# One denominator pass for eight attention heads instead of two passes for four, in a two-layer hybrid decoder trunk

## The chip, the cores and the metric

The kernel runs on one core of one Trainium2 chip. The metric is the device time of one execution in microseconds; of several runs the median is given. PE is the matrix engine, DVE the vector engine, ACT the scalar engine, POOL and SP the other two.

## What is computed

Two layers. Each is a half SwiGLU, a mixer of four branches (sliding-window attention, a short gated convolution, "native sparse attention", retention), and another half SwiGLU. The change touches the softmax of the two attention branches. Cut to it:

```
def masked_softmax(s, mask, sink=None):
    s = jnp.where(mask, s, -inf); m = max(s); (sink: m = max(m, sink))
    p = exp(s - m); denom = sum(p); (sink: denom += exp(sink - m))
    return p / max(denom, 1e-30)

for each block of 128 queries and each of 8 heads (2 groups of 4 heads share keys and values):
    o = masked_softmax(q @ k.T * scale, mask, sink) @ v
merged = sum over branches of sigmoid(gate_i) * (y_i @ W_branch_i);   x = x + merged @ w_out
```

With 512 tokens the selected blocks of the sparse branch are all blocks, so its "selected" and "window" parts are both causal attention over the keys so far, and each is weighted by a gate per head.

## The kernel before

Tokens are four blocks of 128 (`NT`). All large matmuls run as sums of products of a rounded part and a remainder of the operands (`whi`, `wlo` from `split`: ACT makes `whi` at L214, DVE makes `wlo` at L215), so each weight tile costs one ACT and one DVE instruction before PE can use it.

The sliding-window branch (`swa`) calls `soft` once for each token block, the sparse branch (`nsa`) twice for each (selected, then window, with 1 to 4 key blocks), so a layer has 12 calls. For a head, `scores` makes two matmuls into a PSUM bank `sc` (two banks; L1057, L1058), DVE adds the mask, scales and takes the extreme (L1072) into a tile `P` (nine buffers), and ACT takes the exponential and its sum (L1073). The sums of four heads stand in a tile `dn` of 128x4; DVE bounds it (L1080), inverts it (L1082), in `nsa` multiplies it by the gate (L1084), in `swa` first adds the sink's term (L1077 to L1079), and then scales the four P (L1086). This is `soft_g`, called for group 0 and then group 1.

`pv_acc` then transposes P in key blocks (`turn(j)`: four transposes of group 0 into one PSUM bank `tp`, four of group 1 into the other, L1095), ACT copies each bank to a tile `PT` (three buffers, L1099), and PE multiplies by the values into the bank `pv` (L1108). The transposes of a group at j = 0 wait by hand (`together`) for the last scaling of that group. At the end of a token block `put_y` rounds `pv` (ACT, L851) and takes the remainder (DVE, L852).

Which instruction stands where on each engine is decided by a scheduler when the program is built, from priorities in the order of the code and its own estimate of when things are ready. Every engine then works through its fixed order. What fills PE between the steps of the attention is `merge`: gate projections (L232) and branch matmuls (L834), and on DVE L807, L838 and L839 behind them. In `nsa` the work at hand is `merge(3, yd)`, the retention branch. `merge(2, yc)`, the sparse branch itself, can only start when `nsa` has ended, and w_out and the second SwiGLU follow it. Its L834 read `E` (the rounded part, from L851) and `y` (the remainder, from L852).

Of the kernel before, what the change touches and what calls it, by code (L numbers as in the profile page):

```python
# [13 lines left out]
OP = mybir.AluOpType  # L14
# [58 lines left out]
def body(tc, ins, out):  # L73
    nc = tc.nc
    pe, dve, act, pool, sp = nc.tensor, nc.vector, nc.scalar, nc.gpsimd, nc.sync
    L = ins["w_in"].shape[0]
    es = ExitStack()
# [7 lines left out]
    def sc_t():  # L85
        return pp.tile([128, 512], F32, name="sc", tag="sc", bufs=2)

    def tp_t():
        return pp.tile([128, 512], F32, name="tp", tag="tp", bufs=2)
# [75 lines left out]
    def small(shape, dt=F32, name="sm", bufs=6):  # L165
        n = int(np.prod(shape[1:]))
        return (ph.get("mx") or wp).tile([shape[0], n], dt, name=name, tag=name, bufs=bufs)
# [530 lines left out]
    def mixer(l, spill, F):  # L698
# [12 lines left out]
        def p_t():  # L711
            return aq.tile([128, 512], F32, name="P", tag="P", bufs=9)
# [4 lines left out]
        G, o, oq = {}, 0, 0  # L717
        for nm, a in (("swa_q", ins["swa_q_gain"][l]), ("swa_k", ins["swa_k_gain"][l]),
                      ("nsa_q", ins["nsa_q_gain"][l]), ("nsa_k", ins["nsa_k_gain"][l].rearrange("a b -> (a b)")),
                      ("sink", ins["swa_sinks"][l])):  # L720
            n = a.shape[0]
# [10 lines left out]
        nsink = small([128, 8], name="nsink", bufs=1)  # L732
# [20 lines left out]
        mark, pv_last, scaled, ahead = {}, [None], {}, {}  # L753

        def together(first, ready):

            tc.add_manual_dep(first.ins, ready.ins.name, SYNC, reason="together")
# [296 lines left out]
        def scores(i, qT, kT, h, s0, n):  # L1054
            g, q = h // 4, qT[h][:, i * 128:(i + 1) * 128]
            ps = sc_t()
            pe.matmul(ps[:, :n], q, kT[0][:, g, s0:s0 + n], start=True, stop=False)  # L1057
            pe.matmul(ps[:, :n], q, kT[1][:, g, s0:s0 + n], start=False, stop=True)  # L1058
            return ps

        def soft(i, qT, rr, kT, s0, n, mask, wts, sink):

            return [p for g in range(2) for p in soft_g(g, i, qT, rr, kT, s0, n, mask, wts, sink)]

        def soft_g(g, i, qT, rr, kT, s0, n, mask, wts, sink):
            nm = small([128, 4], name="nm", bufs=4)
            dn = small([128, 4], name="dn", bufs=4)
            P = []
            for h in range(4):
                ps = scores(i, qT, kT, 4 * g + h, s0, max(n, 256))  # L1070
                p = p_t()
                dve.tensor_tensor_reduce(p[:, :n], ps[:, :n], mask, rr[:, i, 4 * g + h:4 * g + h + 1], nsink[:, 4 * g + h:4 * g + h + 1] if sink else 3e38, OP.add, OP.min, nm[:, h:h + 1])  # L1072
                act.activation(p[:, :n], p[:, :n], AF.Exp, bias=nm[:, h:h + 1], scale=-1.0, accum_out=dn[:, h:h + 1])  # L1073
                P.append(p)
            if sink:
                e = small([128, 4], name="es", bufs=4)
                dve.tensor_tensor(e, nm, G["sink"][:, 4 * g:4 * g + 4], op=OP.add)  # L1077
                act.activation(e, e, AF.Exp)
                dve.tensor_tensor(dn, dn, e, op=OP.add)  # L1079
            dve.tensor_scalar(dn, dn, 1e-30, None, op0=OP.max)  # L1080
            w = small([128, 4], name="w8", bufs=4)
            dve.reciprocal(w, dn)  # L1082
            if wts is not None:
                dve.tensor_tensor(w, w, wts[:, 4 * g:4 * g + 4], op=OP.mult)  # L1084
            for h in range(4):
                scaled[g] = dve.tensor_scalar(P[h][:, :n], P[h][:, :n], w[:, h:h + 1], None, op0=OP.mult)  # L1086
            return P

        def pv_acc(pv, P, nblk, V, first, last):
            def turn(j):  # L1090
                pts = []
                for g in range(2):
                    ps = tp_t()
                    for r in range(4):
                        t = pe.transpose(ps[:, r * 128:(r + 1) * 128], P[4 * g + r][:, j * 128:(j + 1) * 128], ident)  # L1095
                        if r == 0 and j == 0:
                            together(t, scaled[g])
                    pt = aq.tile([128, 512], F32, name="PT", tag="PT", bufs=3)
                    last_copy[0] = act.activation(pt, ps, AF.Copy)  # L1099
                    pts.append(pt)  # L1100
                return pts, last_copy[0]

            last_copy = [None]
            pts, copied = turn(0)
            for j in range(nblk):
                nxt = turn(j + 1) if j + 1 < nblk else (None, None)
                for g in range(2):
                    pv_last[0] = pe.matmul(pv[g * 64:(g + 1) * 64], V(g, j), pts[g], start=first and j == 0, stop=last and j == nblk - 1)  # L1108
                    if g == 0:

                        together(pv_last[0], copied)
                pts, copied = nxt
# [4 lines left out]
        def swa(qT, rr, V, kT):  # L1117
            y = y_tiles()
            for i in range(NT):
                s0, n = (max(i - 1, 0) * 128, 256 if i else 128)  # L1120
                mask = C["band"] if i else C["band"][:, 128:]
                P = soft(i, qT, rr, kT[0], s0, n, mask, None, True)
                pv = pv_t()
                b0 = max(i - 1, 0)
                pv_acc(pv, P, n // 128, lambda g, j: V(0, g, b0 + j), True, True)
                mark["swa"] = pv_last[0]
                put_y(pv, y, i)
            return y
# [75 lines left out]
        def nsa(gates):  # L1204
# [8 lines left out]
            for i in range(NT):  # L1213
# [35 lines left out]
                for ty in range(2):  # L1249
                    P = soft(i, qT, rr, kT[ty], 0, n, mask, g3[:, i, :, 1 + ty], False)  # L1250
                    pv_acc(pv, P, i + 1, lambda g, j, ty=ty: V(ty, g, j), False, ty == 1)
# [134 lines left out]
    for l in range(L):  # L1386
        E = early(l)
        ffn_run(F, (E,))
        E.go(None, st["made"].ins)
        ph["two"] = False  # L1390
        leave("hp")
        leave("fp")
        F = ffn(*weights(2, l), norm_end, to_next(l))
        mixer(l, spills[l], F)
        enter("hp", "left")
        nxt = ffn(*weights(1, l + 1), norm_end, to_mix(l + 1)) if l < L - 1 else None
        ffn_run(F, nxt)
        F = nxt
# [30 lines left out]
```

## Time and profile before

| what | value |
| --- | --- |
| median of 3 runs | 2732.51 us (2730.71 to 2732.75) |
| profiled execution: time, span | 2731.97 us, 2729.9 us |
| PE busy | 2705.9 us (99%), 17303 matmuls |
| DVE busy | 2086.9 us (76%), 3474 instructions |
| ACT busy | 1346.8 us (49%), 2136 instructions |
| DMA | 291 MB, mean 107 GB/s |

The time is the span plus 2.1 us around it. Busy shares are means over stages that differ: the sliding-window stages lie at about 550 to 610 and 1900 to 1960 us, the sparse-attention stages at 835 to 965 and 2190 to 2315 us, and the rest is the two SwiGLUs, projections and retention. A PE that is busy is not always at its peak, as the ends of matmuls are modelled.

### The profile page before, as it was taken

Reading aid. Unit: us, or ns where it says so; the run is one execution under the profiler, and the core shown is the slowest. Engines: PE = TensorE matmul, PEld = TensorE weight load, DVE = VectorE, ACT = ScalarE, POOL = GpSimd, SP = SyncE. Lnnn points to the kernel's source line nnn. Section 1 sums busy time; section 2 is a strip of 40 time slices with the busy share of each in tenths; the row PEclk is TensorE's granted clock in tenths of the full one; section 3 lists DMA queues with packets and bytes.
Section 4 is the critical chain, followed back from the end, with each engine's and each line's share of the span. In section 5 each row is a group of like instructions: output and inputs, shape, how many; then the busy total and the mean of one; then the engine's idle time right before and its main releaser. Section 6 shows DMA issues by size and latency. Waiting matters only on the chain.

```text
span 2729.9 us, 42548 instructions
## 1 busy us (share of the span) xinstructions
PE 2705.9 (99%) x17303; PEld 2368.0 (87%) x17303; DVE 2086.9 (76%) x3474; ACT 1346.8 (49%) x2136; POOL 65.0 (2%) x70
## 2 busy tenths in 40 slices
PE   8999999999999999999999999999999999999999
PEld 7999999978877679999899999998788776899997
DVE  8887799674858779786897868996658587788774
ACT  7444565463336655443554435655532465554442
POOL 0000010000000010000000000000000000100000
PEclk8999999999999999999999999999999999999999
DMA  5223423523332152323323333344232323332322
GB/s 172 93 89 112 132 97 129 183 83 114 91 124 63 35 182 82 120 86 101 124 78 111 98 101 125 108 154 149 74 110 91 110 62 97 120 109 93 115 72 77
DMA packets 243335, 291.24 MB, mean 107 GB/s; under 512 B 8060, under 2 KB 211652, under 8 KB 241092
## 3 DMA queue, kind: packets, MB, share of 16 engines
q1 hardware_dynamic: 235604, 273.78, 30.8%
q0 software_dynamic: 3136, 12.59, 1.4%
q8 instruction: 135, 2.21, 0.3%
q10 hardware_dynamic: 4400, 2.17, 0.3%
q14 instruction: 60, 0.49, 0.1%
HBM read 269.64 MB, written 18.87 MB: 106 GB/s over the span
## 4 chain that ended last, share of the span: by engine, by line
PE 85%; issue 10%; DVE 2%; ACT 2%; DMA 1%; POOL 0%; ACTq 0%; POOLq 0%; DVEq 0%
PE sc L437 23%; PE mm L567 16%; PE tp L437 12%; PE mm L232 7%; PE pv L437 6%; PE mm L834 5%; PE mm L786 3%; PE mm L1312 3%; PE pv L1108 2%; PE tp L1095 2%; PE sc L1057 1%; PE pv L786 1%; PE sc L1058 1%; DMA rawd<-in_ffn_w_down_dram 0%; PE sc L1158 0%
## 5 line engine op out<-in xcount | busy, mean ns | idle before, releaser
L214 ACT ACTIVATE whi<-raw 128x1024 fp32r<-128x1024 f32 (+2 forms) x338 | 333.7, 989 | 563.8 <-PE mm L567 122.6
L215 DVE TENSOR_TENSOR wlo<-raw,whi 128x1024 fp32r<-128x1024 f32 (+2 forms) x338 | 381.6, 1134 | 160.3 <-ACT whi L214 154.1
L567 PE MATMUL mm<-h,whi 128*128 128x512 f32 x1408 | 442.9, 395 | 0.2 <-DVE h L554 0.2
L214 ACT ACTIVATE whi<-s 128x1024 fp32r<-128x1024 f32 x232 | 245.8, 1060 | 337.6 <-PE tp L437 83.6
L215 DVE TENSOR_TENSOR wlo<-s,whi 128x1024 fp32r<-128x1024 f32 x232 | 282.7, 1220 | 48.6 <-ACT whi L214 48.0
L567 PEld LDWEIGHTS mm<-h,whi 128*128 128x128 f32 x1408 | 259.9, 188 | 59.6 <-DVE h L554 0.6
L437 PE MATMUL sc<-E,whi 128*128 128x256 f32 x1856 | 295.9, 281 | 0.0
L567 PE MATMUL mm<-h,wlo 128*128 128x512 f32 x704 | 277.9, 395 | 0.0
L437 PEld LDWEIGHTS sc<-E,whi 128*128 128x128 f32 x1856 | 253.1, 190 | 0.4 <-ACT sn L424 0.4
L437 PE MATMUL sc<-E,wlo 128*128 128x256 f32 x928 | 186.3, 282 | 0.0
L571 DVE SCALAR_TENSOR_TENSOR XT<-mm,XT 128x512 f32<-128x512 f32 x128 | 88.1, 688 | 124.8 <-PE mm L567 124.8
L437 PE MATMUL sc<-Ahi,whi 128*128 128x256 f32 x816 | 165.5, 284 | 3.3 <-ACT whi L214 3.3
L232 PE MATMUL mm<-Ahi,whi 128*128 128x512 f32 x416 | 165.2, 397 | 0.0
L232 PE MATMUL mm<-Ahi,wlo 128*128 128x512 f32 x416 | 164.7, 396 | 0.0
L437 PE MATMUL sc<-Ahi,wlo 128*128 128x256 f32 x816 | 164.1, 283 | 0.5 <-DVE wlo L215 0.5
L437 PE MATMUL sc<-Alo,whi 128*128 128x256 f32 x816 | 164.2, 283 | 0.0
L232 PE MATMUL mm<-Alo,whi 128*128 128x512 f32 x416 | 164.1, 394 | 0.0
L567 PEld LDWEIGHTS mm<-h,wlo 128*128 128x128 f32 x704 | 132.0, 187 | 32.2
L214 ACT ACTIVATE whi<-rawd 128x1024 fp32r<-128x1024 f32 (+1 forms) x96 | 94.7, 988 | 131.3 <-PE sc L437 66.1
L437 PE MATMUL tp<-E,whi 128*128 128x256 f32 x928 | 148.1, 281 | 0.0
L437 PEld LDWEIGHTS sc<-E,wlo 128*128 128x128 f32 x928 | 143.3, 190 | 0.2 <-DVE wlo L215 0.2
L443 DVE TENSOR_TENSOR s<-s,raw 128x1024 f32<-128x1024 f32 x116 | 141.4, 1219 | 0.9
(321 smaller groups left out, 6036.6 us busy)
## 6 DMA issues: line engine op xcount, KB each, us to landing
raw<-in_w_in_dram SPq DMA_DIRECT2D x66, 1024.0 KB, 5.8
raw<-in_ffn_w_gate_dram SPq DMA_DIRECT2D x44, 1024.0 KB, 5.3
raw<-in_ffn_w_up_dram SPq DMA_DIRECT2D x44, 1024.0 KB, 7.8
rawd<-in_ffn_w_down_dram SPq DMA_DIRECT2D x32, 1024.0 KB, 5.4
rawd<-in_ffn_w_down_dram SPq DMA_DIRECT2D x16, 768.0 KB, 4.4
gs<-O SPq DMA_DIRECT2D x8, 1024.0 KB, 4.0
raw<-in_w_branch_dram SPq DMA_DIRECT2D x8, 1024.0 KB, 7.5
raw<-in_w_branch_dram SPq DMA_DIRECT2D x16, 512.0 KB, 8.8
```

Of the source, the lines that this page charges most:

```text
L214: act.activation(hi, src, AF.Copy)
L215: dve.tensor_tensor(lo, src, fv(hi), op=OP.subtract)
L232: pe.matmul(ps, x, y, start=first and j == 0, stop=last and j == len(passes) - 1)
L437: pe.matmul(ps[:, g * 256:(g + 1) * 256], x[:, g * 4 + c], factor(u, s, c), start=first and n == 0, stop=last and n >= 22, skip_group_chec ...
L443: dve.tensor_tensor(t, a, b, op=OP.add)
L567: pe.matmul(ps, x[:, k, j * 128:(j + 1) * 128], h[:, s, b], start=k == 0 and n == 0, stop=k == nf - 1 and n == 2)
L571: dve.scalar_tensor_tensor(XT[d], ps, 0.5, XT[d], op0=OP.mult, op1=OP.add)
L786: pe.matmul(ps[i][:, :n], a, w, start=kk == 0 and j == 0, stop=kk == KT - 1 and j == 2)
L834: pe.matmul(ps, x[:, k], v[:, k], start=k == 0 and j == 0, stop=k == 3 and j == 2)
L1095: t = pe.transpose(ps[:, r * 128:(r + 1) * 128], P[4 * g + r][:, j * 128:(j + 1) * 128], ident)
L1108: pv_last[0] = pe.matmul(pv[g * 64:(g + 1) * 64], V(g, j), pts[g], start=first and j == 0, stop=last and j == nblk - 1)
L1312: pe.matmul(ps, x[:, k], v, start=k == 0 and j == 0, stop=k == KT - 1 and j == 2)
```

## The change

The maxima, the sums, the reciprocals and the weights of all eight heads of a block now stand in tiles of 128x8. The instructions on them are issued once for eight heads, after the last exponential, and all eight P are scaled behind them. The first transposes of both groups wait for the last of the eight scalings, so the eight of j = 0 stand together. The three small tiles have three buffers in place of four. Below the change the lines of the kernel move up by three (L1095 becomes L1092, L1086 becomes L1083, L1108 becomes L1105).

```diff
         def soft(i, qT, rr, kT, s0, n, mask, wts, sink):
 
-            return [p for g in range(2) for p in soft_g(g, i, qT, rr, kT, s0, n, mask, wts, sink)]
-
-        def soft_g(g, i, qT, rr, kT, s0, n, mask, wts, sink):
-            nm = small([128, 4], name="nm", bufs=4)
-            dn = small([128, 4], name="dn", bufs=4)
+            nm = small([128, 8], name="nm", bufs=3)
+            dn = small([128, 8], name="dn", bufs=3)
             P = []
-            for h in range(4):
-                ps = scores(i, qT, kT, 4 * g + h, s0, max(n, 256))
+            for h in range(8):
+                ps = scores(i, qT, kT, h, s0, max(n, 256))
                 p = p_t()
-                dve.tensor_tensor_reduce(p[:, :n], ps[:, :n], mask, rr[:, i, 4 * g + h:4 * g + h + 1], nsink[:, 4 * g + h:4 * g + h + 1] if sink else 3e38, OP.add, OP.min, nm[:, h:h + 1])
+                dve.tensor_tensor_reduce(p[:, :n], ps[:, :n], mask, rr[:, i, h:h + 1], nsink[:, h:h + 1] if sink else 3e38, OP.add, OP.min, nm[:, h:h + 1])
                 act.activation(p[:, :n], p[:, :n], AF.Exp, bias=nm[:, h:h + 1], scale=-1.0, accum_out=dn[:, h:h + 1])
                 P.append(p)
             if sink:
-                e = small([128, 4], name="es", bufs=4)
-                dve.tensor_tensor(e, nm, G["sink"][:, 4 * g:4 * g + 4], op=OP.add)
+                e = small([128, 8], name="es", bufs=3)
+                dve.tensor_tensor(e, nm, G["sink"], op=OP.add)
                 act.activation(e, e, AF.Exp)
                 dve.tensor_tensor(dn, dn, e, op=OP.add)
             dve.tensor_scalar(dn, dn, 1e-30, None, op0=OP.max)
-            w = small([128, 4], name="w8", bufs=4)
+            w = small([128, 8], name="w8", bufs=3)
             dve.reciprocal(w, dn)
             if wts is not None:
-                dve.tensor_tensor(w, w, wts[:, 4 * g:4 * g + 4], op=OP.mult)
-            for h in range(4):
-                scaled[g] = dve.tensor_scalar(P[h][:, :n], P[h][:, :n], w[:, h:h + 1], None, op0=OP.mult)
+                dve.tensor_tensor(w, w, wts, op=OP.mult)
+            for h in range(8):
+                scaled[h // 4] = dve.tensor_scalar(P[h][:, :n], P[h][:, :n], w[:, h:h + 1], None, op0=OP.mult)
             return P
...
                         if r == 0 and j == 0:
-                            together(t, scaled[g])
+                            together(t, scaled[1])
```

The scheduler orders more than these lines anew. On PE, here is the last block of the sparse branch in layer 1 as it stands before, from the second run of transposes on (`tp<-ident,P` are transposes, `pv` the products with the values, `mm` the merge of the retention branch):

```order
L1095 MATMUL tp<-ident,P 128x128 x8
L232 MATMUL mm<-Ahi,wlo 128x512
L834 MATMUL mm<-E,whi 128x512 x2
L1095 MATMUL tp<-ident,P 128x128 x4
L1108 MATMUL pv<-PT,b_8029 64x512 x2
L1095 MATMUL tp<-ident,P 128x128 x4
L834 MATMUL mm<-E,wlo 128x512
L1095 MATMUL tp<-ident,P 128x128 x4
L1108 MATMUL pv<-PT,b_8029 64x512 x2
L1095 MATMUL tp<-ident,P 128x128 x4
L834 MATMUL mm<-E,whi 128x512
L1095 MATMUL tp<-ident,P 128x128 x4
```

The same place on PE with the change, from the last merge matmuls of the retention branch to the first two of the sparse branch (`y_7567` is its remainder):

```order
L834 MATMUL mm<-E,whi 128x512 x2
L834 MATMUL mm<-E,wlo 128x512
L1092 MATMUL tp<-ident,P 128x128 x16
L1105 MATMUL pv<-PT,b_7993 64x512 x2
L1092 MATMUL tp<-ident,P 128x128 x8
L1105 MATMUL pv<-PT,b_7993 64x512 x2
L1092 MATMUL tp<-ident,P 128x128 x8
L1105 MATMUL pv<-PT,b_7993 64x512 x4
L834 MATMUL mm<-E,whi 128x512
L834 MATMUL mm<-y_7567,whi 128x512
```

The merge matmuls between and behind the transposes are gone from there: all of the retention branch's stand ahead of the first transposes. Counted over the whole order from the last scores of `nsa` to its first merge matmul, 40 merge matmuls (L232, L834) stood there before and 14 do now; the other 26 stand ahead of the last scores. Layer 2 has the same counts.

On DVE, the end of the same block before (`w_9191` holds the weights of the second four heads, `mm` in L838 is a merge product):

```order
L838 SCALAR_TENSOR_TENSOR th<-th,mm 128x512
L839 TENSOR_TENSOR merged<-merged,th 128x512
L1080 TENSOR_SCALAR dn<-dn 128x4
L1082 RECIPROCAL w_9191<-dn 128x4
L1084 TENSOR_TENSOR w_9191<-w_9191,cg 128x4
L1086 TENSOR_SCALAR P<-P,w_9191 128x512 x4
L215 TENSOR_TENSOR wlo<-raw,whi 128x1024
L807 TENSOR_TENSOR th<-mm,R 128x512
L852 TENSOR_TENSOR y_7603<-pv,E 128x4x128
```

And with the change, behind the eighth L1069 (the mask and maximum of the last head, L1072 before):

```order
L807 TENSOR_TENSOR th<-mm,R 128x512
L215 TENSOR_TENSOR wlo<-raw,whi 128x1024
L1077 TENSOR_SCALAR dn<-dn 128x8
L1079 RECIPROCAL w_9103<-dn 128x8
L838 SCALAR_TENSOR_TENSOR th<-th,mm 128x512
L1081 TENSOR_TENSOR w_9103<-w_9103,cg 128x8
L839 TENSOR_TENSOR merged<-merged,th 128x512
L215 TENSOR_TENSOR wlo<-raw,whi 128x1024
L1083 TENSOR_SCALAR P<-P,w_9103 128x512 x8
L852 TENSOR_TENSOR y_7567<-pv,E 128x4x128
```

Between the reciprocals and the scalings now stand L838, L839 and a split of weights. That L838 reads the product `mm` of the last merge matmuls of the retention branch, those ahead of the sixteen transposes.

## Rows read from the trace of the kernel before

**Rows 1.** Busy time by engine in the sparse stage of layer 1.
```profile
core 0: us, PE busy (x) PEld busy (x) DVE busy (x) ACT busy (x) POOL busy (x), PEclk, DMA share, GB/s
835.00:965.00 130.00, 129.24 (x658) 87.34 (x657) 98.39 (x329) 81.75 (x203) 4.52 (x8) 1.00 0.24 68
```

**Rows 2.** Groups by shape: busy us, mean ns, then idle time before them.
```profile
L1082 DVE RECIPROCAL w<-dn 128x4 f32<-128x4 f32 x48 | 8.4, 175 | 0.9
L1080 DVE TENSOR_SCALAR dn<-dn 128x4 f32<-128x4 f32 x48 | 8.0, 166 | 3.6 <-ACT P L1073 3.3
```

**Rows 3.** Timeline, layer 1: last scores to the second transposes; start us, us, engine.
```profile
942.48 0.40 PE L1058 MATMUL sc<-b,b 128*128 128x512 f32 x1
...
943.88 0.60 PE L1095 MATMUL tp<-ident,P 128*128 128x128 f32 x4
...
944.23 0.48 PE L232 MATMUL mm<-Alo,whi 128*128 128x512 f32 x1
...
944.55 0.39 PE L232 MATMUL mm<-Ahi,wlo 128*128 128x512 f32 x1
...
944.78 0.40 PE L232 MATMUL mm<-Ahi,whi 128*128 128x512 f32 x1
...
944.88 0.74 DVE L1072 CUSTOM_DVE_ANT_0 P<-sc,cst,rr 128x512 f32<-128x512 f32 x1
...
947.49 1.67 DVE L1086 TENSOR_SCALAR P<-P,w 128x512 f32<-128x512 f32 x4
...
949.34 1.04 PE L1095 MATMUL tp<-ident,P 128*128 128x128 f32 x8
...
950.13 0.48 PE L232 MATMUL mm<-Ahi,wlo 128*128 128x512 f32 x1
...
950.45 0.63 PE L834 MATMUL mm<-E,whi 128*128 128x512 f32 x2
```

**Rows 4.** Timeline, layer 1: first product with the values to the first sparse merge.
```profile
951.72 1.08 PE L1108 MATMUL pv<-PT,b 128*64 128x512 f32 x4
...
952.89 0.60 ACT L1099 ACTIVATE PT<-tp 128x512 f32<-128x512 f32 x1 [1.32 <-PE pv L1108]
...
953.54 0.66 PE L1095 MATMUL tp<-ident,P 128*128 128x128 f32 x4
...
958.44 1.08 PE L1108 MATMUL pv<-PT,b 128*64 128x512 f32 x4
...
961.16 0.50 PE L834 MATMUL mm<-E,whi 128*128 128x512 f32 x1 [0.28 <-ACT whi L214]
```

**Rows 5.** Groups by shape in 940 to 962 us, as in rows 2.
```profile
L214 ACT ACTIVATE whi<-raw 128x1024 fp32r<-128x1024 f32 x4 | 4.0, 1050 | 3.1 <-PE mm L232 3.1
...
L215 DVE TENSOR_TENSOR wlo<-raw,whi 128x1024 fp32r<-128x1024 f32 x2 | 2.4, 1222 | 1.5 <-ACT whi L214 1.5
L838 DVE SCALAR_TENSOR_TENSOR th<-th,mm 128x512 f32<-128x512 f32 x2 | 1.4, 684 | 0.0
L839 DVE TENSOR_TENSOR merged<-merged,th 128x512 f32<-128x512 f32 x1 | 0.7, 692 | 0.0
```

**Rows 6.** Timeline, layer 2: last scores, last values, rounding, first sparse merge.
```profile
2291.63 0.39 PE L1058 MATMUL sc<-b,b 128*128 128x512 f32 x1
...
2307.59 1.08 PE L1108 MATMUL pv<-PT,b 128*64 128x512 f32 x4
...
2308.72 0.60 ACT L851 ACTIVATE E<-pv 128x512 fp32r<-128x512 f32 x1 [1.27 <-PE pv L1108]
...
2309.87 0.61 PE L834 MATMUL mm<-E,whi 128*128 128x512 f32 x2
```

**Rows 7.** Busy time and clock as in rows 1, at both ends of the run.
```profile
10.00:12.00 2.00, 0.47 (x3) 0.14 (x1) 2.00 (x5) 2.00 (x6) 0.00 (x0) 1.00 1.04 340
12.00:14.00 2.00, 1.43 (x7) 1.29 (x8) 1.68 (x7) 2.00 (x6) 0.00 (x0) 0.63 0.97 299
26.00:28.00 2.00, 2.00 (x18) 2.00 (x18) 2.00 (x5) 1.27 (x3) 0.00 (x0) 0.95 0.00 0
2728.00:2729.90 1.90, 0.00 (x0) 0.00 (x0) 0.00 (x0) 0.00 (x0) 0.00 (x0) 0.91 0.18 47
```

## The prediction, made before the changed kernel ran

> **What bounds the kernel now.** I read the windows by stage first, then the order of the changed program on PE and DVE, then the timeline at the one place where the two orders differ in kind. The reader should see in [rows 1] that PE sets the pace of the stage that the change edits: in 130 us of the sparse stage PE is busy for 129.24 us, DVE for 98.39, ACT for 81.75. The attention itself could not keep PE that busy; the merge of the retention branch does, one matmul after another in every gap. One such matmul costs 0.23 us (944.55 to 944.78) [rows 3]. So the supply of these matmuls is the resource of this stage. It is finite: when it is used up, PE has nothing to do until `nsa` has ended, since the merge of the sparse branch needs the result of the last token block.
>
> Before, the supply lasted to the end. From the last scores in layer 1 (942.48) to the first matmul of the sparse merge (961.16) [rows 3, 4] it is 18.68 us, with 40 merge matmuls in it by the order, 9.2 us of PE's time. In layer 2 it is 2291.63 to 2309.87, 18.24 us [rows 6].
>
> **The change part by part.**
>
> *Fewer small instructions.* 24 calls lose one L1080 and one L1082 each, the 16 of `nsa` an L1084, the 8 of `swa` an L1077 and an L1079: 80 instructions on DVE. At 0.17 us each, the mean of L1080 and L1082 [rows 2] taken for all, that is 13.6 us of DVE, with ACT losing 8 small exponentials besides. I count it at nothing: it lies under the merge matmuls on PE [rows 1]. If that cover were gone, in the last block of a layer, the eight-wide instructions still stand in the chain once, and I count them there. The price lies between 0 and 13.6 us of gain; near 0, because DVE idles for a quarter of the stage already.
>
> *Eight transposes in one run.* Four alone take 0.35 us to the next matmul's start (943.88 to 944.23), and that one then 0.32 in place of 0.23 us; eight in a run take 0.79 and then 0.32 (949.34, 950.13, 950.45) [rows 3]. So 0.35 + 0.09 = 0.44 for four alone, against 0.44 for each half of the run of eight. One switch less saves nothing. What the run adds is that a third group of four finds both `tp` banks taken and waits for ACT's copies; that was so before as well, with the groups parted otherwise. I take 0, between -0.1 and +0.1 us a call, 2.4 us either way.
>
> *The first transposes wait for eight scalings.* This is the large part. Before, PE could transpose group 0 while group 1 was still in its exponentials. Now the first transpose of a call comes behind all eight. The scheduler fills the longer wait with merge matmuls while it has some. That by itself costs nothing, as they have to run anyway. But by the counts, 26 more of them have been spent when the last scores of `nsa` start (14 left in place of 40), so those scores start 26 x 0.23 = 6.0 us later, and the end of the layer's attention has lost its cover. I now follow that end in the new order, with t = 0 at the last L1058.
>
> PE: 14 merge matmuls, done with the last result at about t = 3.7 (14 x 0.23, plus 0.4 for the last to end). DVE: the last mask and maximum needs 0.74 us (944.88) [rows 3] and starts at about 0.5; then L807 (0.69, taken like L838 [rows 5]), a split of 1.22 whose `whi` takes ACT 1.05 [rows 5], and two small ones, which reaches t = 3.9. Next on DVE is L838, which reads the last of those 14 products: ready at about the same time. Behind it are queued, in this order: L838 0.68, L1081 0.17, L839 0.69, the split L215 1.22, eight scalings at 1.67 for four (947.49), 3.34 [rows 3, 5]. With 3.9 as the start that is 3.9 + 6.1 = 10.0, and 0.1 for the signal: sixteen transposes start at t = 10.1. PE has been without work since 3.5, **about 6.6 us**, and everything on PE is queued behind these transposes.
>
> From the first transposes of a run to the first product with the values I take what it is now, 949.34 to 951.72, 2.4 us [rows 3, 4]: there too it waits for the copies. From the first to the last of the four products it is 951.72 to 958.44, 6.7 us [rows 4]. This does not shrink without the merge matmuls in it: the copy starts 1.17 us after the product (952.89), as it needs one of three PT buffers, and the next transposes start behind it (953.54). Then layer 1 needs 958.44 to 961.16, 2.7 us [rows 4], for the rounding and a split that comes behind it on ACT; in the new order of layer 1 the same split stands behind the rounding. In the new order of layer 2 that split is done earlier, so I take the rounding alone: 2307.59 to 2308.72, plus 0.60, plus 0.1, 1.8 us [rows 6].
>
> So layer 1 takes 10.1 + 2.4 + 6.7 + 2.7 = 21.9 us where it took 18.68, and layer 2 10.1 + 2.4 + 6.7 + 1.8 = 21.0 where it took 18.24: 3.2 and 2.8 us more, with 26 matmuls less in each. With the 6.0 us by which each starts late, the layers lose 9.2 and 8.8 us: **18.0 us**. The sliding-window stages also wait for eight scalings, but behind them PE has the projections of retention to go on with: 0.
>
> *The clock.* [...] At the start of the run the level fell in 12 to 14 us (mean 0.63), after a stretch in which PE was busy for 0.47 us of 2, and was back up in 26 to 28 us; at the end it fell in 2728 to 2729.9 us, when PE had no work [rows 7]. No row shows a gap of 6.6 us inside the run. [...] At half the level PE does half the work, so 4 us at the lower level cost at most 2 us. Bounds for a layer: 0, if it doesn't fall, or if the waits for copies hide it; 7, half of the 14 us between the fall and the return at the start. I take 2, as PE is at work without a break there and was not at the start: 4 us in both layers.
>
> [...]
>
> Sum: 18.0 + 4 = 22 us on the profiled execution's own time of 2731.97 us (span 2729.9 and 2.1 around it): **2754 us**. That execution lies 0.5 us under the median of the runs shown, so the same sum holds for the median.
>
> **The rivals.**
>
> *The gap comes, the clock stays up.* For it: no gap of this kind in the middle of the run is on record. Against it: both falls of [rows 7]. 18 us: 2750.
>
> *The clock stays down long.* As at the start of the run, 14 us in each layer: 18 + 14 = 32, 2764. Against it: there PE had hardly any work after the fall, here it has.
>
> *The gap is much smaller.* If ACT and DVE, with 6.8 us less of small instructions in each layer, are further ahead than I take it, L838 still can't start before PE's 14 matmuls end, and the 6.1 us behind it remain. So the gap can only shrink if the six microseconds of delay ahead of it are not real, because PE waited in the blocks before for scores and loses those waits now. That would give about 8 to 10 us in all, 2741. [Rows 1] leave PE 0.76 us of such waits in a layer by busy time.
>
> *Relief of DVE decides, and the kernel gets faster.* It would take PE waiting for the small instructions in most of the 24 calls: then half to all of 13.6 us come back, 2718 to 2725. It decides from the point at which DVE's relief per layer, 6.8 us, exceeds the loss at the layer's end; [rows 1] speak against it, as PE has less than 1 us of idle time in the stage to give back. [...]
>
> *The change does nothing that can be measured.* The scheduler might have found other work for the gap. The order shows none: 2732.
>
> **How the numbers follow.** 0.2% is 5.5 us, about what a measurement of this kernel tells from no change. The forecast (gap and fall of the clock) 0.53; clock stays up 0.22; clock long down 0.07; smaller gap 0.08; same 0.05; faster 0.05. Slower is 0.53 + 0.22 + 0.07 + 0.08 = 0.90. The likeliest case gives 2754. The range goes from 2740, below the smaller gap, to 2764, the clock long down; it leaves out the two cases of 0.05 and the margin above.
>
> **What would show it.** In the profile after: a wait of PE of 6 to 7 us in each layer, at about 950 and 2310 us, ahead of L1092 and ended by DVE's scaling L1083 of P; the sixteen transposes right behind it; L838, L839 and L215 on DVE inside that gap; PEclk under 1.00 in the stretch behind it; the last L1057 of layer 1 at about 948, where it was at 942; PE's busy time the same but for slower matmuls; 80 instructions less on DVE. Wrong would be: no wait over 2 us there; or waits of PE for scores before, spread over all calls, that have gone. If the gap is there and the time isn't, work lost there has been regained in the merge and w_out behind it.

## The result and the profile after

The change makes the kernel slower. The median is 2753.47 us (2752.55 to 2754.32, 4 runs) where the kernel before took 2732.61 us (2730.71 to 2732.75, 4 runs): a ratio of 1.0077, 95% interval 1.0066 to 1.0089, or 20.9 us more. The profiled execution took 2752.55 us, its span grew from 2729.9 to 2750.8.

The first lines of the page after:

```profile
span 2750.8 us, 42487 instructions
## 1 busy us (share of the span) xinstructions
PE 2709.9 (99%) x17303; PEld 2371.7 (86%) x17303; DVE 2080.0 (76%) x3394; ACT 1345.8 (49%) x2128; POOL 64.6 (2%) x70
```

PE has the same 17303 matmuls and 4.0 us more busy time, though the kernel takes 20.9 us longer. DVE has the 80 instructions less. Neither says where the time is. The windows do: the stage of [rows 1], then two-microsecond pieces behind the last scores of layer 1 and of layer 2.

```profile
core 0: us, PE busy (x) PEld busy (x) DVE busy (x) ACT busy (x) POOL busy (x), PEclk, DMA share, GB/s
835.00:965.00 130.00, 123.48 (x621) 84.56 (x621) 92.99 (x301) 77.36 (x196) 4.29 (x8) 0.97 0.23 65
954.00:956.00 2.00, 0.00 (x0) 0.00 (x0) 2.00 (x6) 0.00 (x0) 0.44 (x1) 1.00 0.88 313
956.00:958.00 2.00, 0.22 (x1) 0.26 (x2) 1.63 (x5) 0.00 (x0) 0.00 (x0) 0.56 0.79 299
958.00:960.00 2.00, 2.00 (x10) 1.71 (x10) 0.00 (x0) 0.78 (x2) 0.00 (x0) 0.50 0.06 25
...
964.00:966.00 2.00, 1.91 (x11) 0.93 (x12) 0.00 (x0) 0.79 (x3) 0.00 (x0) 1.00 0.03 8
2314.00:2316.00 2.00, 0.00 (x0) 0.00 (x0) 2.00 (x5) 0.00 (x0) 1.15 (x3) 0.69 0.84 289
```

PE was busy for 129.24 of these 130 us [rows 1] and is now for 123.48. At 954 to 956 it does nothing while DVE works without a break; then the granted clock falls to 0.50 and is back at 1.00 by 964 to 966. In layer 2 it has fallen already in 2314 to 2316, while PE is still idle.

The timeline of layer 1 from the last scores on, to be read beside [rows 3, 4]; a bracket is the idle time of the engine and what ended it:

```profile
948.21 0.40 PE L1058 MATMUL sc<-b,b 128*128 128x512 f32 x1
...
951.42 0.39 PE L834 MATMUL mm<-E,wlo 128*128 128x512 f32 x1
...
951.91 0.69 DVE L838 SCALAR_TENSOR_TENSOR th<-th,mm 128x512 f32<-128x512 f32 x1
...
952.64 0.69 DVE L839 TENSOR_TENSOR merged<-merged,th 128x512 f32<-128x512 f32 x1
953.25 1.22 DVE L215 TENSOR_TENSOR wlo<-raw,whi 128x1024 fp32r<-128x1024 f32 x1
954.38 3.25 DVE L1083 TENSOR_SCALAR P<-P,w 128x512 f32<-128x512 f32 x8
...
957.78 3.80 PE L1092 MATMUL tp<-ident,P 128*128 128x128 f32 x16 [5.97 <-DVE P L1083]
...
961.51 1.84 PE L1105 MATMUL pv<-PT,b 128*64 128x512 f32 x4
...
968.91 1.08 PE L1105 MATMUL pv<-PT,b 128*64 128x512 f32 x4 [0.74 <-ACT PT L1096]
...
971.63 0.50 PE L834 MATMUL mm<-E,whi 128*128 128x512 f32 x1 [1.64 <-ACT whi L214]
```

The last scores stand at 948.21, before at 942.48. PE has its last merge matmul of retention at 951.42 and then waits 5.97 us for the scalings, which stand on DVE behind L838, L839 and a split. Layer 2 has the same gap (beside [rows 6]):

```profile
2308.92 0.40 PE L1058 MATMUL sc<-b,b 128*128 128x512 f32 x1
...
2318.48 3.53 PE L1092 MATMUL tp<-ident,P 128*128 128x128 f32 x16 [5.97 <-DVE P L1083]
2321.94 1.08 PE L1105 MATMUL pv<-PT,b 128*64 128x512 f32 x4
...
2328.57 1.08 PE L1105 MATMUL pv<-PT,b 128*64 128x512 f32 x4 [0.74 <-ACT PT L1096]
2330.34 0.50 PE L834 MATMUL mm<-E,whi 128*128 128x512 f32 x1 [0.70 <-ACT E L851]
```

The first sparse merge comes 971.63 - 961.16 = 10.5 us later in layer 1 and 2330.34 - 2309.87 = 20.5 us later in layer 2. That is the whole loss of the span but 0.4 us.

### The profile page after: what moved, and what is told of

The parts are those of the page before. It is cut to its first block, busy times and chain, and to the rows that moved or that the text cites. A ratio compares the mean times of both kernels' runs of the same rounds, so it can differ in the third digit from the quotient of the medians.

```text
span 2750.8 us, 42487 instructions
## 1 busy us (share of the span) xinstructions
PE 2709.9 (99%) x17303; PEld 2371.7 (86%) x17303; DVE 2080.0 (76%) x3394; ACT 1345.8 (49%) x2128; POOL 64.6 (2%) x70
## 4 chain that ended last, share of the span: by engine, by line
PE 83%; issue 10%; DVE 4%; ACT 2%; DMA 1%; POOL 0%; ACTq 0%; POOLq 0%; DVEq 0%
PE sc L437 22%; PE mm L567 16%; PE tp L437 11%; PE mm L232 7%; PE pv L437 5%; PE mm L834 5%; PE mm L786 3%; PE mm L1309 3%; PE pv L1105 2%; PE tp L1092 2%; PE sc L1057 1%; PE pv L786 1%; DVE wlo L215 1%; PE sc L1058 1%; DMA rawd<-in_ffn_w_down_dram 1%
## 5 line engine op out<-in xcount | busy, mean ns | idle before, releaser
L214 ACT ACTIVATE whi<-raw 128x1024 fp32r<-128x1024 f32 (+2 forms) x338 | 333.9, 989 | 545.1 <-PE mm L567 122.8
L214 ACT ACTIVATE whi<-s 128x1024 fp32r<-128x1024 f32 x232 | 245.9, 1060 | 337.2 <-PE tp L437 78.1
L232 PE MATMUL mm<-Alo,whi 128*128 128x512 f32 x416 | 164.8, 396 | 0.0
L232 PE MATMUL mm<-Ahi,whi 128*128 128x512 f32 x416 | 164.7, 396 | 0.0
L232 PE MATMUL mm<-Ahi,wlo 128*128 128x512 f32 x416 | 163.8, 394 | 0.0
L214 ACT ACTIVATE whi<-rawd 128x1024 fp32r<-128x1024 f32 (+1 forms) x96 | 94.7, 988 | 132.2 <-PE sc L437 66.3
```

The costliest lines, as they stand in the source:

```text
L214: act.activation(hi, src, AF.Copy)
L232: pe.matmul(ps, x, y, start=first and j == 0, stop=last and j == len(passes) - 1)
```

## The experiments

Every ratio is to the kernel before as measured beside the kernel in question; its median lay between 2732.05 and 2732.72 us. So differences between kernels of different parts of this section are good to about 0.6 us.

**The theory:** PE has a finite supply of merge matmuls in a sparse stage. Longer waits for scalings in all its calls use it up sooner, so the last call of the layer stands without cover; there DVE's queue makes the gap, and the clock that falls in it adds some. **Rival 1:** each of the 24 calls pays alike, 0.87 us. **Rival 2:** the single pass, or the wait for eight scalings, is itself the cost. **Rival 3,** on the gap alone: it can't be used, or isn't DVE's queue.

### The sliding-window calls alone, and the sparse calls alone

The softmax of the kernel before (`soft_g`, left out below) stands again beside the new one and is called where `one[0]` is false:

```diff
         def soft(i, qT, rr, kT, s0, n, mask, wts, sink):
+            one[0] = sink        # the other kernel: not sink
+            if not one[0]:
+                return [p for g in range(2) for p in soft_g(g, i, qT, rr, kT, s0, n, mask, wts, sink)]
...
-                            together(t, scaled[1])
+                            together(t, scaled[1] if one[0] else scaled[g])
```

> The change is made in the sliding-window branch alone (8 of the 24 calls); the sparse branch keeps its two passes. In the trace of the changed kernel PE has no gap of 6 us behind the sliding-window calls, only 2 us or less, since the projections of retention stand there. Theory (the loss sits at the end of each sparse stage, where the merge matmuls that cover the wait are used up): 2732 us, between 2730 and 2734. Rival (every call with eight at once pays alike, 20.9 us / 24 = 0.87 us each): 8 x 0.87 = 7 us more, 2739.5.

> The change is made in the sparse branch alone (16 of the 24 calls); the sliding-window branch keeps its two passes. Theory (the loss sits at the ends of the two sparse stages): the whole loss, 2753 us, between 2751 and 2755, with a gap of 6 us on PE ahead of the sixteen transposes in both layers. Rival (every call pays alike): 16 x 0.87 = 14 us more, 2746.5.

Measured: in the sliding-window branch alone 2733.15 us, ratio 1.0002 (0.9992 to 1.0011); in the sparse branch alone 2752.88 us, ratio 1.0074 (1.0059 to 1.0089). The whole loss is in the sparse calls, and rival 1 misses by 6 us both ways.

### Only the last call of a layer, and all calls but those of the last block

The same predicate, in the sparse branch true only in the window part of the last token block, or everywhere but in that block:

```diff
-            one[0] = sink
+            one[0] = last_call[0]            # i == NT - 1 and ty == 1
...
-            one[0] = sink
+            one[0] = sink or i < NT - 1
```

> In the sparse branch all eight at once only in the very last call of each layer (window part, last token block); the other seven calls of a layer and the sliding-window branch keep two passes. By the order on PE 36 merge matmuls then stand between the last scores and the sparse merge (40 before, 14 with the whole change), spread between the transposes. Theory (what costs is that the cover was spent earlier, by the wait for eight scalings in all the calls before; with the cover there the same wait in the last call is filled): (40-36) x 0.23 = 1 us late per layer and no gap over 2 us, 2733 to 2737. Rival A (the wait for eight scalings in the last call is itself the loss, wherever the merge matmuls stand): the gap of 6 us and its clock remain, 2748 or more. Rival B (every call pays alike): 2 x 0.87 = 1.7, 2734, which this run cannot tell from the theory.

> All eight at once everywhere but in the two calls of the last token block of the sparse branch, which keep two passes. By the order 17 merge matmuls stand between the last scores and the sparse merge (14 with the whole change, 40 before). Theory (spent cover): the last scores still start 23 x 0.23 = 5.3 us late per layer; what the end of the layer then loses is less, because group 0 can be transposed while group 1 is still being scaled; I estimate 10 us in all for both layers, 2743, between 2738 and 2748. Rival A (the wait in the last calls is itself the loss): no loss is left, 2733. Rival B (every call pays alike): 20 x 0.87 = 17.4, 2750.

Measured: the last call alone 2733.80 us, ratio 1.0004 (0.9994 to 1.0013); all but the last block 2741.98 us, ratio 1.0032 (1.0020 to 1.0045). The first, timeline of layer 1 on PE:

```profile
942.77 0.39 PE L1058 MATMUL sc<-b,b 128*128 128x512 f32 x1
...
949.39 0.39 PE L834 MATMUL mm<-E,whi 128*128 128x512 f32 x1
949.92 1.06 PE L1121 MATMUL tp<-ident,P 128*128 128x128 f32 x8
```

The transposes start 7.2 us behind the last scores, as they wait for all eight, but merge matmuls stand there to the end and PE loses next to nothing. So the call in which the gap shows isn't the one that causes it. The second, same view:

```profile
948.66 0.40 PE L1058 MATMUL sc<-b,b 128*128 128x512 f32 x1
...
955.30 1.06 PE L1121 MATMUL tp<-ident,P 128*128 128x128 f32 x8 [1.89 <-DVE P L1112]
```

Here the last block is as before, yet 9 us are lost: its last scores come 6.2 us later, 17 merge matmuls are left, and PE waits 1.89 us. This decides between the theory (2743) and rivals 1 (2750) and 2 (2733).

### The wait without the single pass

The kernel before with one line changed; and the changed kernel with the same line changed back:

```diff
-                            together(t, scaled[g])
+                            together(t, scaled[1])
```

> The kernel before (denominators in two passes of four) with one edit: the first transposes of both groups wait for the last scaling of the second group. All the small instructions of before are there. By the order 11 merge matmuls stand between the last scores and the sparse merge (40 before, 14 with the change). Theory (the wait of the first transposes for all eight scalings spends the cover, not the number of small instructions): 29 x 0.23 = 6.7 us late per layer, and a gap on PE behind the last scores that is shorter by the four scalings of group 0, which here are done early; 2749 to 2754. Rival (the single pass of denominators is the cost, by coming after the last exponential): this kernel is as fast as before, 2732.

> The changed kernel with one edit: the first transposes of a group wait for the scalings of their own group, not for the last of all eight; denominators stay at once for eight heads. By the order 19 merge matmuls stand between the last scores and the sparse merge (14 with the change, 40 before); the transposes of both groups still stand in one run of sixteen, and on DVE four scalings stand on either side of a split. Theory: (40-19) x 0.23 = 4.8 us late per layer, a gap of 4 to 6 us ahead of the transposes, 2743 to 2749. Rival (the wait for eight scalings, or the run of sixteen that follows from it, is the whole cost): 2732 if the wait alone counts.

Measured: two passes with the wait for all eight 2752.01 us, ratio 1.0073 (1.0058 to 1.0088); one pass with a wait for the own group 2749.32 us, ratio 1.0063 (1.0048 to 1.0078). So the wait alone costs about what the change costs, with every small instruction of before in place. But undoing the wait alone brings back only 4 us (3.6 by the losses against the kernel before beside each), since with a single pass no scaling can start before the last exponential. One part of these expectations failed: I thought that the gap with two passes would be shorter, because four scalings are done early. The timeline, layer 1:

```profile
948.53 0.39 PE L1058 MATMUL sc<-b,b 128*128 128x512 f32 x1
...
951.40 0.75 DVE L1072 CUSTOM_DVE_ANT_0 P<-sc,cst,rr 128x512 f32<-128x512 f32 x1
...
955.70 1.67 DVE L1086 TENSOR_SCALAR P<-P,w 128x512 f32<-128x512 f32 x4
...
957.52 3.80 PE L1095 MATMUL tp<-ident,P 128*128 128x128 f32 x16 [6.07 <-DVE P L1086]
```

The early scalings, with a split of 1.22 us among them, stand on DVE ahead of the last maximum, which now starts 2.9 us behind the last scores (0.4 in the changed kernel). What the scalings save at the end is lost there.

The own-group kernel was 0.3 us above the range that I had given. It waits in two pieces, 1.49 and 2.09 us, and 0.31 for a copy, and its products behind them take 967.33 - 959.80 = 7.53 us, in part at the lower clock (0.50 in 960 to 962), as in the changed kernel:

```profile
954.66 0.63 PE L1092 MATMUL tp<-ident,P 128*128 128x128 f32 x4 [1.49 <-DVE P L1083]
957.38 1.06 PE L1092 MATMUL tp<-ident,P 128*128 128x128 f32 x8 [2.09 <-DVE P L1083]
...
959.80 1.98 PE L1105 MATMUL pv<-PT,b 128*64 128x512 f32 x4
...
967.33 1.08 PE L1105 MATMUL pv<-PT,b 128*64 128x512 f32 x4 [0.74 <-ACT PT L1096]
```

### What the gap is made of

The changed kernel with L838, L839 and the sparse merge's first splits issued behind the scalings:

```diff
-                            two = split(raw[:, :, s * 128:(s + 2) * 128], (4, 256))
+                            with tc.issue_after(scaled[1].ins) if b == 2 else ExitStack():
+                                two = split(raw[:, :, s * 128:(s + 2) * 128], (4, 256))
...
+                        with tc.issue_after(scaled[1].ins) if (b, d) == (3, KT - 1) else ExitStack():
+                            dve.scalar_tensor_tensor(z, z, 1.0, ps, op0=OP.add, op1=OP.mult)
+                            dve.tensor_tensor(merged[:, d], merged[:, d], z, op=OP.add)
```

> The changed kernel with one edit: at the end of the sparse stage L838 and L839 of the last merge of retention, and the first split of the sparse merge's weights, are issued after the last scaling. PE's order is that of the changed kernel (14 merge matmuls, then sixteen transposes), so the last scores still start 6.0 us late; on DVE the scalings come right behind the small instructions. Theory (of the 6.0 us of gap about 2.7 us is DVE working through L838, L839 and the split ahead of the scalings): the sixteen transposes start at about 6.9 us behind the last L1058 in place of 9.6, the gap falls from 6.0 to about 3.2 us, and both layers together gain 5 to 7 us, 2746 to 2748 (2744 if the clock then stays up). Rival (the gap is the exponentials and the scalings themselves, or what is put off is lost behind): no gain over 1 us, 2753.

And the changed kernel with useless work in the gap:

```diff
         merge(3, yd, False)
+        for k in range(24):
+            pe.matmul(sc_t(), yd[0][:, k % 4, :128], yd[0][:, k % 4], start=True, stop=True)
```

> The changed kernel with 24 useless matmuls of 128x512 in each layer, put on PE between the last merge matmul of retention and the sixteen transposes, where PE has no work for 6.0 us; nothing is left out. Theory (PE is free there, and the clock falls because it is): 24 x 0.23 = 5.5 us of work fit into the gap at no cost, the granted clock stays at 1.00 behind it, and the 2.0 us (layer 1) and 1.1 us (layer 2) that the transposes and products lose to the lower level come back: 2750, between 2749 and 2752. Rival A (the products behind the gap wait for copies, not for the clock): 2753, with the clock at 1.00. Rival B (PE's work counts even there): 11 us more, 2764.

Measured: scalings first 2747.88 us, ratio 1.0058 (1.0043 to 1.0073); useless matmuls 2750.86 us, ratio 1.0068 (1.0051 to 1.0085). The first, layer 1:

```profile
949.00 0.39 PE L1060 MATMUL sc<-b,b 128*128 128x512 f32 x1
...
952.46 3.26 DVE L1085 TENSOR_SCALAR P<-P,w 128x512 f32<-128x512 f32 x8
...
955.86 3.80 PE L1094 MATMUL tp<-ident,P 128*128 128x128 f32 x16 [3.26 <-DVE P L1085]
```

The transposes start 6.86 us behind the last scores (expected 6.9) and the gap is 3.26 us (3.2). So 2.7 us of the 5.97 were DVE's queue of merge work. The other 3.3 us are the chain itself: mask, exponential, denominators, eight scalings. Even there some 0.8 us is ACT's queue: the last maximum ends at 950.2, but ACT works on the `whi` of a split (L214, from 950.03) and starts the last exponential at 950.98. No run moved that one. The second, on PE, and its windows:

```profile
949.00 0.40 PE L1058 MATMUL sc<-b,b 128*128 128x512 f32 x1
...
952.44 6.76 PE L1269 MATMUL sc<-E 128*128 128x512 f32 x24
959.04 1.04 PE L1092 MATMUL tp<-ident,P 128*128 128x128 f32 x8
...
961.46 1.08 PE L1105 MATMUL pv<-PT,b 128*64 128x512 f32 x4
...
968.09 1.08 PE L1105 MATMUL pv<-PT,b 128*64 128x512 f32 x4 [0.74 <-ACT PT L1096]
```

```profile
956.00:958.00 2.00, 2.00 (x9) 1.31 (x8) 2.00 (x7) 0.00 (x0) 0.00 (x0) 1.00 0.87 311
958.00:960.00 2.00, 2.00 (x13) 1.53 (x12) 0.43 (x2) 0.27 (x1) 0.00 (x0) 1.00 0.46 182
```

With 24 matmuls more in each layer the kernel is 2.6 us faster than the changed one (2.1 by the losses against the kernel before beside each). The gap held some 6 us of work for nothing, the clock stayed at 1.00 through the transposes and products, and the first transposes to the last products take 968.09 - 959.04 = 9.05 us in place of 968.91 - 957.78 = 11.13. This prices the clock: 2.1 us in layer 1, and 10.09 - 9.05 = 1.0 us in layer 2. The transposes start 10.0 us behind the last scores (949.00) where it was 9.57, because the 24 took 959.04 - 952.44 = 6.6 us, 0.28 each, where I had put 0.23.

In layer 1 of the profiled execution, though, the clock only fell later, when PE had waited 1.64 us for the first weights of the sparse merge (at 970.81):

```profile
972.00:974.00 2.00, 2.00 (x6) 1.54 (x5) 1.15 (x2) 0.00 (x0) 0.00 (x0) 0.50 0.38 79
```

It was back at 1.00 in 976 to 978. The ten merge matmuls from 970.81 to 974.79 took 4.0 us, where ten at 0.23 take 2.3. In layer 2 it stayed at 1.00 (the mean of 2190 to 2325 us). So that execution, 2751.76 us and the slowest of its four, isn't one with the clock up all the way.

### Is the supply finite, or only badly placed?

The changed kernel with 24 merge matmuls held back for the last call; and the kernel before, softmax untouched, with the same 24 held back until `nsa` has ended:

```diff
-                    for k in range(4):
+                    with tc.issue_after(mark["score"].ins) if b == 3 and d >= KT - 2 else ExitStack():
+                        for k in range(4):
...
-                    for k in range(4):
+                    with tc.issue_after(pv_last[0].ins) if b == 3 and d >= KT - 2 else ExitStack():
+                        for k in range(4):
```

> The changed kernel with one edit: the last 24 merge matmuls of the retention branch (those of L834 for the last two of its eight column blocks) are held back until the last scores of the sparse branch. By the order 34 merge matmuls then stand behind the last scores (14 with the change, 35 counted in the same way before) and fill the last call as they did before; but the call before it has none left, its sixteen transposes stand right behind its last scores. Theory (every call of this stage waits for its eight scalings in earnest, and the merge matmuls are a finite supply: wherever it runs out, PE stands): the last call loses nothing any more, a gap of 3 to 5 us appears ahead of the sixteen transposes of the call before it, and the products and transposes behind that wait for copies; 2742 to 2750. Rival (the calls before did not need the matmuls, the scheduler spent them there for nothing): no gap over 1 us, 2733 to 2736.

> The kernel before, its softmax in two passes and its waits untouched, with one edit: the last 24 merge matmuls of the retention branch may only be issued behind the last product of the sparse branch with the values; by the order the others behind them move along, and no merge matmul is left in the last two calls of a layer. Theory (the cover, not the softmax, is what the end of the layer lives on): without it PE stands in the last two calls, I estimate 4 us in the last and 2 us in the one before it for each layer, and 1 to 2 us for the clock, 2744 to 2750, between 2738 and 2752. Rival (what costs is the one pass for eight heads, or its wait, as such): as fast as before, 2732.

Measured: held back for the last call 2749.07 us, ratio 1.0063 (1.0048 to 1.0078); the kernel before without that cover 2753.07 us, ratio 1.0076 (1.0059 to 1.0093). The first, layer 1 on PE:

```profile
935.19 3.83 PE L1093 MATMUL tp<-ident,P 128*128 128x128 f32 x16 [3.68 <-DVE P L1084]
...
949.73 0.40 PE L1059 MATMUL sc<-b,b 128*128 128x512 f32 x1
...
956.56 1.06 PE L1093 MATMUL tp<-ident,P 128*128 128x128 f32 x8
...
965.74 1.08 PE L1106 MATMUL pv<-PT,b 128*64 128x512 f32 x4
```

The last call is whole again: 965.74 - 949.73 = 16.0 us from the last scores to the last products, as before (942.48 to 958.44 [rows 3, 4]). The gap has moved one call ahead, 3.68 us at 935, and 17 of the 21 us stay lost. So the call ahead did need its matmuls. This is one other placement; no run tells whether a better one exists. The second, same view:

```profile
942.46 0.40 PE L1059 MATMUL sc<-b,b 128*128 128x512 f32 x1
944.55 0.75 PE L1096 MATMUL tp<-ident,P 128*128 128x128 f32 x4 [1.69 <-DVE P L1087]
949.16 2.95 PE L1096 MATMUL tp<-ident,P 128*128 128x128 f32 x12 [3.87 <-DVE P L1087]
```

With its scores on time and its softmax in two passes the kernel before loses as much as the changed one once the cover is gone. It lost 3 us more than my estimate, 1 us over its range, and not where I had put it. The two gaps, 1.69 and 3.87 us, and the lower clock (0.50 in 948 to 954) are all in the last call. The call before it still had merge matmuls ahead of its transposes of 930.43 and then waited only for copies, 0.53 us and twice 0.15, where I had put 2 us.

No kernel here beats the one before; those that equal it (the sliding-window calls alone, the last call alone) save nothing.

## Why the prediction was right

2754 us was forecast, 2753.47 measured; as a loss, 22 us against 20.9, since the forecast started from an execution 0.6 us under the median. By its own terms, in us, from the rows above and [rows 3, 4, 6]; the loss of layer 1 is taken out of layer 2's first line (2308.92 - 2291.63 - 10.47):

| term | layer 1: forecast, measured | layer 2: forecast, measured |
| --- | --- | --- |
| last scores later | 6.0, 5.73 | 6.0, 6.82 |
| last scores to sixteen transposes | 10.1, 9.57 | 10.1, 9.56 |
| these to the first product | 2.4, 3.73 | 2.4, 3.46 |
| first to last product | 6.7, 7.40 | 6.7, 6.63 |
| last product to sparse merge | 2.7, 2.72 | 1.8, 1.77 |
| clock | 2, in the two lines above it | 2, in the same lines |
| less the time before | 18.68 | 18.24 |
| loss | 11.2, 10.47 | 10.8, 10.00 |

- *Fewer small instructions, counted at nothing:* right. DVE lost its 80 instructions (the small ones of the softmax take 13.9 us in place of 26.5), and the eight-wide ones cost hardly more than the four-wide of [rows 2], as this grouping of the kernel after shows:

```profile
L1079 DVE RECIPROCAL w<-dn 128x8 f32<-128x8 f32 x24 | 4.8, 200 | 0.5
L1077 DVE TENSOR_SCALAR dn<-dn 128x8 f32<-128x8 f32 x24 | 3.9, 164 | 1.8 <-ACT P L1070 1.6
```

  The reciprocal took 200 ns for 128x8 and 175 for 128x4, the lower bound on the sums (L1077, before L1080) 164 and 166. The work that it frees isn't on the path: the sliding-window calls alone, with 32 of the 80 instructions less and no loss at the end, took 2733.15 us, no different from before.
- *Eight transposes in a run at nothing:* no run isolates it. The calls with the sliding window show no price, and at the end of a layer the 2.42 us below, with the clock up, are no more than the 2.4 of before.
- *26 merge matmuls spent early:* right in size (5.7 and 6.8 for 6.0) and in kind, by the two runs on the supply. Counted from the first scores of each sparse branch (839.09 before and 838.54 after; 2188.20 and 2199.17), the last ones come 6.3 us later in both layers: what layer 1 has under this and layer 2 over it arose outside the sparse stages.
- *The new order at the end, gap of 6.6 us:* 5.97. L838 started at t = 3.7 (3.9 forecast, though the pieces named for it, 0.5 + 0.74 + 0.69 + 1.22 + 2 x 0.17, come to 3.5 only), and from it to the end of the scalings DVE took 957.63 - 951.91 = 5.7 us in place of 6.1, since in the rows neighbours on DVE overlap by about 0.1 us.
- *2.4 and 6.7 us for the rest of the layer:* 2.42 and 6.63 where the clock stayed up (useless matmuls in the gap, 1.00 in 958 to 966). So nothing but the clock was added.
- *Clock, 4 us:* the fall was right, the size a little high: 2.1 and 1.0. In layer 2 more of the slow stretch lay in the gap, where PE had nothing to do (2314 to 2318 us: PE busy 0.00, clock 0.69 and then 0.50). The 2 us for a layer rested on a fall to half the level, which no row shown ahead of the forecast has (the lowest is 0.63, the mean of 2 us), and on my guess of 4 us for it: no run shows that term. What the runs showed in its place is 0.50 in 958 to 962 (and in 14 to 26 us of the kernel before), and the 2.1 and 1.0 us. Four products with the values took 1.98 us at 0.50 (own-group kernel, 959.80) and 1.08 at 1.00 (changed kernel, 968.91). In layer 1 the level fell behind 4 us in which PE was busy for 0.00 (952 to 956) and returned under the transposes and products (0.73 in 962 to 964, then 1.00). What makes it fall was not shown, only that with useless matmuls in that gap it stayed at 1.00 there.
- *The rivals:* a clock that stays up would have given about 2750: 2753.47 less the 3.1 us priced above. It didn't stay down long either: it was back at 1.00 by 964 to 966 and by 2322 to 2324. The smaller gap (2741) needed waits of PE for scores in the blocks before, which would then be lost; before the change the only wait of PE in 835 to 965 is one of 0.3 us, for `whi`, and the last scores did come late by 6 us. The relief of DVE never came to the path.

Two of the terms erred to the same side, the gap and the clock by about 1 us each, and the late start of layer 2 to the other. So part of the closeness is luck; the range of 24 us tells better what the working was worth.

## What to carry to other kernels

Where one stage fills another's waits, count the filling work as a stock: what a change adds to each wait is paid at the place where the stock runs out, not where the wait grew. Count in the new order how much of it stands behind the last step that needs it, and follow the engine's queue there by hand; that count told most of a loss of 21 us that no share of busy time showed. Joining small instructions over more heads saved nothing here, on an engine that isn't the bound, and it delays the first head's result to that of the last.

## What the hardware showed that I had not expected

The lower clock cost as much behind a shorter gap: with the scalings first PE was idle for 3.26 us in place of 5.97, and transposes to last products still took 967.12 - 955.86 = 11.26 us (11.13 in the changed kernel), where 9.05 us is the time at 1.00 (useless matmuls in the gap). Layer 2 is alike, 10.0 us (10.09). The windows of that kernel, layer 1:

```profile
954.00:956.00 2.00, 0.14 (x1) 0.17 (x2) 2.00 (x6) 0.00 (x0) 1.97 (x3) 0.75 0.88 274
956.00:958.00 2.00, 2.00 (x10) 1.71 (x11) 2.00 (x3) 0.70 (x2) 0.00 (x0) 0.50 0.96 334
```

In the kernel whose last block kept two passes PE waited 1.89 us at the same place and the granted clock stayed at 1.00, while with the useless matmuls it fell behind a wait of 1.64 us that followed on short ones: the length of the last gap alone doesn't tell. A second thing: sixteen transposes in a run took 957.78 to 961.51, 3.7 us to the first product, at the lower level (0.50 in 958 to 962), and 2.42 us with useless matmuls ahead of them, at the upper (1.00 in 958 to 962).
